# An attention stage whose engines take their work in the stated order

## Chip, cores and metric

The kernel runs on one core of one Trainium2 chip. The metric is the device time of one execution in microseconds. TensorE (PE) multiplies, VectorE (DVE) and ScalarE (ACT) do elementwise work, GpSimd (POOL) clears tiles, and SyncE (SP) issues the loads. The kernel before took 1140.14 us (median of three runs, 1138.94 to 1140.86).

## What is computed

One layer of a hybrid encoder on 256 frames of width 2048, in float32:

```
proj = x @ w_in                      # q | k | v | u, 1024 columns each
attn = chunk_band_attention(q, k, v) # 16 heads of 64; 64-frame chunks, own chunk and 8 before, a bias by distance
s_t  = a * s_(t-1) + B u_t           # 64 groups of 16 channels, a 64-dim complex diagonal state each
ssm  = Re(C s) + D u                 # then gelu, then ssm * sigmoid(ssm @ w_glu + b_glu)
x    = LN(alpha * x + concat(rms(attn), rms(ssm)) @ w_out)
x    = LN(alpha * x + (gelu(conv3(x @ W_gate)) * (x @ W_val)) @ w_ffn_out)
```

## The kernel before

Every large product is made in split form. A weight tile of 128 x 1024 float32 (a *chunk*, 512 KB) is loaded on SP's queue into `raw` (`dma_chunk`, four buffers); ScalarE rounds it to `hi`, VectorE makes `lo = raw - hi` (`split_chunk`, lines 163 and 164, four buffers each); TensorE multiplies hi and lo with activations split in the same way.

Phase 1 consists of 104 chunks, in this order: 0 to 7 half of v, 8 to 23 u, 24 to 31 the other half of v, 32 to 63 k and q (four chunks for each of eight head pairs j: two for k, two for q), 64 to 79 the half of the output projection (`oa`) that takes attention's output, 80 to 87 the gate of the state-space branch (`glu`), 88 to 103 the other half of the output projection (`os`). Phase 2 is the feed-forward part, 176 and 88 chunks.

`run` states the work in steps. Step j states the split of chunk j+3, the load of chunk j+7, the products of chunk j, what copies a finished result out (`evac_k`, `evac_q`: a ScalarE copy of one half and a VectorE addition), and then lets each *side* that has started go on to its next `yield`. Sides are Python generators with a first step; the ones that matter here are, in the order in which a step asks them:

- `s5_loc`, from step 16: the input products of the recurrence. For each of four groups of state columns (`pg`), `lt` transposes coefficients and `ll` (line 778) makes 32 small products of 64 columns; a ScalarE copy takes them into `X`.
- `s5_kstack`, from step 24: the correction products (line 873) and the table `Kt` made of them. `s5_cm`, from step 22: the output matrices `CM`, eight blocks of four VectorE operations (lines 943 to 948, the last doubled).
- `s5_scan`, from step 35: the recurrence in time, 21 complex multiply-adds (`madd`) of four VectorE operations each (lines 844 to 847). `paced` lets whole multiply-adds through until 1.6 us are reached per step. It ends with `s5_y`: four groups of output products (line 973, 32 x 64 pieces) and copies to `ysh`, then gelu and a split.
- `attention(j)`, one side for each head pair, from step 36 + 4j: scores (`S`, lines 1048 and 1049) from `kz` and `qt`, which have one buffer each; softmax (`soft`, VectorE lines 1061 and 1062, ScalarE line 1065); transposes (`T`, lines 1071 to 1073) and a ScalarE copy into `pT` (line 1075; a tile of a pool with one buffer); value products (`O`, lines 1084 to 1086); normalisation (`at`, line 1094, and ScalarE squares, line 1099); `evac`: transposes (line 1104), two ScalarE copies and a subtraction (lines 1108 to 1110) into `attnhl`, the split activations of the output projection. The bias tiles `band` come in two buffers.

Small products that are to fill TensorE's stream go through `queue`: `put(f, cost)` appends one, and `fill`, called between main products, earns one unit of credit (two at most) and takes products while it has a unit left. With cost 0.25 that is four at a time.

The stated order is not the order on the engines. Each instruction has a priority by its place, and a scheduler goes through a model of the engines' times: whenever an engine is free there, it takes the ready instruction of the best priority. So the recurrence, for one, can be put on VectorE earlier than it is stated. On the chip each engine then takes its list strictly in turn. An instruction can also be given an order edge (`add_manual_dep` without a semaphore), which fixes its place behind another one.

Of the kernel before, what the change touches and what calls it, by code (L numbers as in the profile page):

```python
# [34 lines left out]
NEG = -1e30  # L35

# [82 lines left out]
class Builder:  # L119
    def __init__(self, nc, tc, ctx, I, out):  # L120
        self.nc, self.tc, self.ctx, self.I, self.out = nc, tc, ctx, I, out
        self.chunks = []
        self.sides = []
        self.queue = deque()
        self.credit = 0.0
# [41 lines left out]
    def run(self, first=None):  # L167
# [11 lines left out]
        while j < len(self.chunks) or self.sides:  # L179
            self.split_chunk(j + 3)  # L180
# [15 lines left out]
            self.sides = keep  # L196
            j += 1

# [93 lines left out]
    def plan_phase1(self):  # L292
# [165 lines left out]
        self.side(35, self.s5_scan())  # L458
        for j in range(8):
            self.side(36 + 4 * j, self.attention(j))  # L460
# [291 lines left out]
    def s5_loc(self):  # L752
# [20 lines left out]
        def ll(q, ri):  # L773
# [11 lines left out]
            for i in range(8):  # L785
                for g2 in range(2):
                    put(lambda i=i, g2=g2: mm(i, g2), 0.25)
# [32 lines left out]
        both(ll, 2)  # L820
        both(ll, 3)
# [4 lines left out]
    def s5_scan(self):  # L826
# [8 lines left out]
        def madd(cost, o, s, ar, ai, shape, add=None):  # L835
# [4 lines left out]
            def f():  # L840
# [3 lines left out]
                V.tensor_tensor(u, s[:, ::-1], ai, op=ALU.mult)  # L844
                V.tensor_tensor(w, s, ar, op=ALU.mult)
                V.tensor_tensor(u, u, add, op=ALU.add)
                V.tensor_tensor(o, w, u, op=ALU.add)
            ops.append((cost, f))
# [4 lines left out]
        for k in range(2, 9):  # L853
            madd(2.7, row(k), row(k - 1), bc(QR, 0), bc(QI, 0), sh)
        for b in range(7):
            madd(1.1, X[:, :, :, 0, b + 1], X[:, :, :, 0, b], one(QR, 7), one(QI, 7), [P, 2, NP_], L8[:, :, :, b])
        for k in range(1, 8):
            madd(2.7, row(k), row(0), bc(QR, k - 1), bc(QI, k - 1), sh)
        yield from self.paced(ops, 1.6)
        yield from self.s5_y()  # L860

    def s5_kstack(self):
# [14 lines left out]
        for i in range(16):  # L877
            for ri in range(2):
                for h in range(2):
                    self.put(lambda i=i, ri=ri, h=h: mm(i, ri, h), 0.5)  # L880
# [71 lines left out]
    def s5_y(self):  # L952
        nc, bp = self.nc, self.bp
        X, Kt, CM, up = self.X, self.Kt, self.CM, self.up
        for pg in range(4):
# [5 lines left out]
            for f in range(2):  # L961
                for i in range(4):
                    m = slice(32 * i, 32 * i + 32)
                    for t in range(3):
                        for r in range(4):
# [7 lines left out]
                            nc.tensor.matmul(o, start=t == 0, stop=t == 2, tile_position=(0, 32 * r), **a)  # L973
                nc.vector.tensor_copy(ysh[:, 2 * pg + f].rearrange("p (b k i) -> p i k b", i=4, k=8),
# [61 lines left out]
    def attention(self, j):  # L1036
# [5 lines left out]
        def load(h):  # L1042
            b = st["b", h] = ap.tile([P, 256], F32, tag="band", bufs=2, name=f"bd{j}{h}")
            nc.sync.dma_start(b, I["band"][2 * j + h])

# [5 lines left out]
        def soft(h):  # L1051

            ps, b = st["S", h], st["b", h]
# [14 lines left out]
        def trans(h):  # L1068
            s = st["s", h]
            ps = self.bank(7, f"T{j}{h}")  # L1070
# [30 lines left out]
        def evac():  # L1101
# [7 lines left out]
            nc.scalar.copy(self.attnhl[:, j, 0:SEQ], a)  # L1109
# [279 lines left out]
```

## Time and profile before

| | us |
|---|---|
| median of three runs | 1140.14 |
| the profiled execution | 1141.15 |
| its span, first to last instruction | 1139.3 |
| busy: PE, DVE, ACT, POOL | 1110.3, 774.4, 566.6, 75.5 |
| mean granted TensorE clock | 0.991 |
| start of chunk 36 and of chunk 75 | 133.56, 301.04 |

In a row of a timeline the first number is the start in us from the span's start, the second the length, then engine, line, operation, out<-in by the program's names, shapes and a count; in brackets stands the idle time of the engine before it, and what ended that. Where a matmul's row is longer than the distance to the next start, the two overlap in the pipeline: the distance between starts is the price. A row of a table by stretches has the stretch, its length, the busy time of PE, PEld (weight loads), DVE, ACT and POOL with their instruction counts, the granted clock of TensorE (1.00 is full), the share of the DMA engines and GB/s. "[1.52 <-PE kq L209]" means that the engine was idle for 1.52 us and that a product of k or q at line 209 ended it.

### The profile page before, as it was taken

Reading aid. Unit: us, or ns where it says so; the run is one execution under the profiler, and the core shown is the slowest. Engines: PE = TensorE matmul, PEld = TensorE weight load, DVE = VectorE, ACT = ScalarE, POOL = GpSimd, SP = SyncE. Lnnn points to the kernel's source line nnn. Section 1 sums busy time; section 2 is a strip of 40 time slices with the busy share of each in tenths; the row PEclk is TensorE's granted clock in tenths of the full one; section 3 lists DMA queues with packets and bytes.
Section 4 is the critical chain, followed back from the end, with each engine's and each line's share of the span. In section 5 each row is a group of like instructions: output and inputs, shape, how many; then the busy total and the mean of one; then the engine's idle time right before and its main releaser. Section 6 shows DMA issues by size and latency. Waiting matters only on the chain.

```text
span 1139.3 us, 17905 instructions
## 1 busy us (share of the span) xinstructions
PE 1110.3 (97%) x6980; PEld 948.8 (83%) x6980; DVE 774.4 (68%) x1230; ACT 566.6 (50%) x882; POOL 75.5 (7%) x75
## 2 busy tenths in 40 slices
PE   8999979999999999999999999999999999999996
PEld 6887768888887888888888888888888888888885
DVE  7996889946588776666666666666666575454555
ACT  5455325537575565555555555555555443433350
POOL 2021300000011000000000000000000550000002
PEclk9999979999999999999999999999999999999998
DMA  8886334534766366666666666666666876666661
GB/s 303 279 226 164 118 122 139 162 96 138 244 188 201 108 204 186 185 188 185 188 188 188 186 187 186 186 185 185 189 186 187 307 223 197 190 198 190 192 195 74
DMA packets 61572, 212.03 MB, mean 186 GB/s; under 512 B 7344, under 2 KB 10800, under 8 KB 60592
## 3 DMA queue, kind: packets, MB, share of 16 engines
q1 hardware_dynamic: 59728, 204.18, 58.9%
q0 software_dynamic: 1472, 6.29, 1.8%
q8 instruction: 54, 0.88, 0.3%
q10 hardware_dynamic: 288, 0.43, 0.1%
q14 instruction: 30, 0.25, 0.1%
HBM read 207.46 MB, written 3.41 MB: 185 GB/s over the span
## 4 chain that ended last, share of the span: by engine, by line
PE 93%; DVE 4%; ACT 1%; issue 1%; DMA 1%; SPq 0%; POOL 0%; ACTq 0%; POOLq 0%
PE f L231 29%; PE f L224 15%; PE d L245 7%; PE d L249 7%; PE d L247 7%; PE kq L209 5%; PE u L209 2%; PE kq L211 2%; PE oa L249 1%; PE oa L245 1%; PE oa L247 1%; PE u L211 1%; PE glu L209 1%; DVE lo L164 1%; PE os L249 1%; PE os L245 1%
## 5 line engine op out<-in xcount | busy, mean ns | idle before, releaser
L164 DVE TENSOR_TENSOR lo<-raw,hi 128x1024 fp32r<-128x1024 f32 (+1 forms) x358 | 446.3, 1249 | 210.6 <-ACT hi L163 207.0
L163 ACT CAST hi<-raw 128x1024 fp32r<-128x1024 f32 (+1 forms) x358 | 374.3, 1047 | 300.0 <-PE d L249 116.9
L231 PE MATMUL f<-x1s,hi 128*128 128x512 f32 (+1 forms) x1408 | 487.2, 396 | 1.5 <-DVE x1s L1211 1.5
L224 PE MATMUL f<-x1s,lo 128*128 128x256 f32 x1408 | 380.0, 281 | 0.0
L231 PEld LDWEIGHTS f<-x1s,hi 128*128 128x128 f32 x1408 | 258.8, 188 | 57.6 <-DVE x1s L1211 1.8
L224 PEld LDWEIGHTS f<-x1s,lo 128*128 128x128 f32 x1408 | 265.8, 189 | 8.6
L247 PE MATMUL d<-lo,hid 128*128 128x512 f32 (+1 forms) x360 | 133.4, 371 | 0.0
L245 PE MATMUL d<-hi,hid 128*128 128x512 f32 (+1 forms) x360 | 133.4, 370 | 0.0
L249 PE MATMUL d<-hi,hid 128*128 128x512 f32 (+1 forms) x360 | 133.3, 370 | 0.0
L209 PE MATMUL kq<-xs,hi 128*128 128x512 f32 x240 | 92.8, 422 | 5.1 <-DVE qt L506 2.6
L247 PEld LDWEIGHTS d<-lo,hid 128*128 128x128 f32 x360 | 67.9, 188 | 11.7
L249 PEld LDWEIGHTS d<-hi,hid 128*128 128x128 f32 x360 | 67.8, 188 | 11.7
L245 PEld LDWEIGHTS d<-hi,hid 128*128 128x128 f32 x360 | 67.9, 188 | 11.5
L211 PE MATMUL kq<-xs,lo 128*128 128x256 f32 x240 | 69.8, 291 | 0.0
L209 PEld LDWEIGHTS kq<-xs,hi 128*128 128x128 f32 x240 | 47.0, 196 | 15.8 <-DVE qt L506 2.7
L1319 ACT COPY ga<-f 128x256 f32<-128x256 f32 x44 | 16.4, 372 | 83.3 <-PE f L231 83.3
L1326 DVE TENSOR_TENSOR gp<-f,ga 128x256 f32<-128x256 f32 x44 | 18.8, 426 | 45.6 <-ACT ga L1319 45.6
L1319 ACT COPY va<-f 128x256 f32<-128x256 f32 x44 | 16.4, 372 | 66.1 <-PE f L231 66.1
L1338 DVE TENSOR_TENSOR va<-f,va 128x256 f32<-128x256 f32 x44 | 18.7, 425 | 43.0 <-ACT va L1319 43.0
L211 PEld LDWEIGHTS kq<-xs,lo 128*128 128x128 f32 x240 | 47.2, 197 | 0.8
L209 PE MATMUL u<-xs,hi 128*128 128x512 f32 x120 | 43.5, 401 | 0.0
L1305 POOL DMA_DIRECT2D gb<-rows x4 | 2.2, 554 | 531.6 <-PE f L231 531.6
(228 smaller groups left out, 1366.9 us busy)
## 6 DMA issues: line engine op xcount, KB each, us to landing
raw<-wf SPq DMA_DIRECT2D x176, 512.0 KB, 3.7
raw<-wd SPq DMA_DIRECT2D x88, 512.0 KB, 4.1
raw<-wkq SPq DMA_DIRECT2D x32, 512.0 KB, 3.7
raw<-wo SPq DMA_DIRECT2D x32, 512.0 KB, 4.0
raw<-wu SPq DMA_DIRECT2D x16, 512.0 KB, 4.7
raw<-wv SPq DMA_DIRECT2D x15, 512.0 KB, 6.2
raw<-wg SPq DMA_DIRECT2D x8, 512.0 KB, 3.7
gb<-rows POOLq DMA_DIRECT2D x4, 1024.0 KB, 13.1
```

The source lines that it names most:

```text
L163: self.nc.scalar.copy(hi[:, c], raw[:, c])
L164: self.nc.vector.tensor_tensor(lo[:, c], raw[:, c], hi[:, c].bitcast(F32), op=ALU.subtract)
L209: nc.tensor.matmul(ps, start=first and kk == 0, stop=False, **h)
L211: nc.tensor.matmul(ps[:, 0:SEQ], start=False, stop=False, **l)
L224: nc.tensor.matmul(th(ps), lhsT=lo[:, w], rhs=th(x), start=False, stop=False)
L231: nc.tensor.matmul(ps[:, c], lhsT=hi[:, w], rhs=x[:, c], start=start and part is None, stop=stop)
L245: nc.tensor.matmul(ps, lhsT=ah, rhs=wh, start=first and kk == 0, stop=False)
L247: nc.tensor.matmul(ps, lhsT=ah, rhs=wl, start=False, stop=False)
L249: nc.tensor.matmul(ps, lhsT=al, rhs=wh, start=False, stop=last and kk == 1)
L1319: self.nc.scalar.copy(tv, v[:, :, 1])
L1326: nc.vector.tensor_tensor(g[:, 2:].rearrange("p (t c) -> p t c", t=2), p0, t, op=ALU.add)
L1338: nc.vector.tensor_tensor(tv, p0, tv, op=ALU.add)
```

## The change

In steps 36 to 73 every instruction of PE, DVE and ACT gets an order edge to the one stated before it on the same engine (`keep_order`, called at the end of each step), so that these three take their work as stated. SP and POOL are left to the scheduler. With it:

- The recurrence is spread out: single VectorE operations instead of whole multiply-adds, 1.2 us of them (0.68 or 0.28 each) per step up to step 63 and 2.4 from step 64. It is stated to end in step 69, and so the state's output products are stated in steps 70 to 73, among the chunks of the output projection.
- The 64-column products come in runs: the input products and the correction products cost 0 in the queue, the last two groups of input products are separated, and in `s5_y` both halves of a group are multiplied before the two copies.
- Attention's steps are drawn together: scores and softmax of both heads in the first step, both transposes two steps later (the second in bank 6, or 4 for the last pair), both value products and the normalisation in the next, then `evac`, its subtraction a step later. The bias tiles of a pair are loaded a pair ahead.

```diff
--- before.py
+++ after.py
@@ -33,6 +33,7 @@
 EPS = 1e-5
 ALPHA = 2.0 ** 0.25
 NEG = -1e30
+PINNED = 36, 74
 
 NPP = 8 + 8 + 8 + 16 + 16 + 44 * 4
 
@@ -122,6 +123,7 @@
         self.chunks = []
         self.sides = []
         self.queue = deque()
+        self.mark, self.last = None, {}
         self.credit = 0.0
 
 
@@ -177,6 +179,7 @@
         self.start()
         j = 0
         while j < len(self.chunks) or self.sides:
+            self.j = j
             self.split_chunk(j + 3)
             self.dma_chunk(j + 7)
             if j < len(self.chunks):
@@ -194,7 +197,28 @@
                         continue
                 keep.append(s)
             self.sides = keep
+            if first is not None:
+                self.keep_order(PINNED[0] <= j < PINNED[1])
             j += 1
+
+    def keep_order(self, on):
+
+        new, mark = [], self.mark
+        for i in reversed(self.nc.cur_bb.bb.instructions):
+            if i is mark:
+                break
+            new.append(i)
+        if new:
+            self.mark = new[0]
+        if not on:
+            return
+        for i in reversed(new):
+            if i.engine in (mybir.EngineType.PE, mybir.EngineType.DVE, mybir.EngineType.Activation):
+                prev = self.last.get(i.engine)
+                if prev is not None:
+                    self.tc.add_manual_dep(i, prev, mybir.DependencyInfo(
+                        mybir.DependencyClass.NoSync, mybir.DependencyReason.DATA), reason="order")
+                self.last[i.engine] = i.name
 
 
     def mm_a(self, ps, hi, lo, xs, k0, first, last, nk=8):
@@ -456,6 +480,7 @@
         self.side(24, self.s5_kstack(), 200)
         self.side(22, self.s5_cm())
         self.side(35, self.s5_scan())
+        self.side(30, self.first_band())
         for j in range(8):
             self.side(36 + 4 * j, self.attention(j))
         self.side(78, self.load_x())
@@ -784,7 +809,7 @@
                 nc.scalar.copy(self.L8[:, ri, q * 8:q * 8 + 8], v[:, :, 56:64])
             for i in range(8):
                 for g2 in range(2):
-                    put(lambda i=i, g2=g2: mm(i, g2), 0.25)
+                    put(lambda i=i, g2=g2: mm(i, g2), 0)
             put(evac, 0)
 
         def both(f, pg):
@@ -818,6 +843,7 @@
             yield
         yield
         both(ll, 2)
+        yield from drained()
         both(ll, 3)
         yield from drained()
         self.loc_done = True
@@ -841,22 +867,30 @@
                 u, w = (self.kcm[:, c:c + n].rearrange("p (r x) -> p r x", r=2) for c in (1024, 1536))
                 if len(shape) == 4:
                     u, w = (t.rearrange("p r (c b) -> p r c b", b=shape[3]) for t in (u, w))
-                V.tensor_tensor(u, s[:, ::-1], ai, op=ALU.mult)
-                V.tensor_tensor(w, s, ar, op=ALU.mult)
-                V.tensor_tensor(u, u, add, op=ALU.add)
-                V.tensor_tensor(o, w, u, op=ALU.add)
-            ops.append((cost, f))
+                return ((u, s[:, ::-1], ai, ALU.mult), (w, s, ar, ALU.mult), (u, u, add, ALU.add), (o, w, u, ALU.add))
+            for i in range(4):
+                def g(i=i):
+                    d, a, b, op = f()[i]
+                    V.tensor_tensor(d, a, b, op=op)
+                ops.append((cost, g))
         sh = [P, 2, NP_, 8]
         one = lambda q, k: q[:, :, :, k]
         bc = lambda q, k: one(q, k).unsqueeze(3).broadcast_to(sh)
         row = lambda k: L8 if k == 8 else X[:, :, :, k]
         for k in range(2, 9):
-            madd(2.7, row(k), row(k - 1), bc(QR, 0), bc(QI, 0), sh)
+            madd(0.68, row(k), row(k - 1), bc(QR, 0), bc(QI, 0), sh)
         for b in range(7):
-            madd(1.1, X[:, :, :, 0, b + 1], X[:, :, :, 0, b], one(QR, 7), one(QI, 7), [P, 2, NP_], L8[:, :, :, b])
+            madd(0.28, X[:, :, :, 0, b + 1], X[:, :, :, 0, b], one(QR, 7), one(QI, 7), [P, 2, NP_], L8[:, :, :, b])
         for k in range(1, 8):
-            madd(2.7, row(k), row(0), bc(QR, k - 1), bc(QI, k - 1), sh)
-        yield from self.paced(ops, 1.6)
+            madd(0.68, row(k), row(0), bc(QR, k - 1), bc(QI, k - 1), sh)
+        have = 0.0
+        for cost, f in ops:
+            while have < cost:
+                yield
+                have += 1.2 if self.j < 64 else 2.4
+            f()
+            have -= cost
+        yield
         yield from self.s5_y()
 
     def s5_kstack(self):
@@ -877,7 +911,7 @@
         for i in range(16):
             for ri in range(2):
                 for h in range(2):
-                    self.put(lambda i=i, ri=ri, h=h: mm(i, ri, h), 0.5)
+                    self.put(lambda i=i, ri=ri, h=h: mm(i, ri, h), 0)
         while self.queue:
             yield
         ps = st[0]
@@ -971,6 +1005,7 @@
                             else:
                                 a = dict(lhsT=CM[pg][:, t - 1, l, m], rhs=X[:, t - 1, pr])
                             nc.tensor.matmul(o, start=t == 0, stop=t == 2, tile_position=(0, 32 * r), **a)
+            for f in range(2):
                 nc.vector.tensor_copy(ysh[:, 2 * pg + f].rearrange("p (b k i) -> p i k b", i=4, k=8),
                                       ps[:, f * SEQ:(f + 1) * SEQ].rearrange("p (i k b) -> p i k b", i=4, k=8))
             yield
@@ -1039,10 +1074,6 @@
         v = self.res1
         st = {}
 
-        def load(h):
-            b = st["b", h] = ap.tile([P, 256], F32, tag="band", bufs=2, name=f"bd{j}{h}")
-            nc.sync.dma_start(b, I["band"][2 * j + h])
-
         def scores(h):
             ps = st["S", h] = self.bank(5 + h, f"S{j}{h}")
             nc.tensor.matmul(ps[:, 0:256], lhsT=qt[:, P:2 * P], rhs=kz[h], start=True, stop=True)
@@ -1050,7 +1081,7 @@
 
         def soft(h):
 
-            ps, b = st["S", h], st["b", h]
+            ps, b = st["S", h], self.band[j, h]
             s = ap.tile([P, 384], F32, tag="sT", bufs=2, name=f"sT{j}{h}")
             if h == 0:
                 st["m"] = ap.tile([P, 12], F32, tag="mx", bufs=2, name=f"mx{j}")
@@ -1067,7 +1098,7 @@
 
         def trans(h):
             s = st["s", h]
-            ps = self.bank(7, f"T{j}{h}")
+            ps = self.bank((7, 6 if j < 7 else 4)[h], f"T{j}{h}")
             nc.tensor.transpose(ps[:, 0:128], s[:, 256:384], self.ident)
             nc.tensor.transpose(ps[:, 128:256], s[:, 0:128], self.ident)
             nc.tensor.transpose(ps[:, 256:384], s[:, 128:256], self.ident)
@@ -1107,31 +1138,35 @@
             a = self.t1([P, SEQ], f"ag{j}")
             nc.scalar.mul(a, ps, self.pv["g_attn"][:, j:j + 1])
             nc.scalar.copy(self.attnhl[:, j, 0:SEQ], a)
+            yield
             nc.vector.tensor_tensor(self.attnhl[:, j, SEQ:], a, self.attnhl[:, j, 0:SEQ].bitcast(F32), op=ALU.subtract)
 
-        load(0)
-        load(1)
         scores(0)
         scores(1)
-        yield
         soft(0)
-        yield
         soft(1)
-        yield
         if j < 7:
-            yield
+            self.load_band(j + 1)
+        yield
+        yield
         trans(0)
+        trans(1)
         yield
         pv(0)
-        trans(1)
-        if j < 7:
-            yield
         pv(1)
         norm()
         yield
-        while self.cm_ready < 4:
-            yield
-        evac()
+        assert self.cm_ready == 4
+        yield from evac()
+
+    def load_band(self, j):
+        for h in range(2):
+            b = self.band[j, h] = self.ap_.tile([P, 256], F32, tag="band", bufs=2, name=f"bd{j}{h}")
+            self.nc.sync.dma_start(b, self.I["band"][2 * j + h])
+
+    def first_band(self):
+        self.band = {}
+        self.load_band(0)
         yield
 
 

```

More of the change, by code (lines that the diff above doesn't have):

```diff
@@ L1109, in evac @@
             nc.scalar.copy(self.attnhl[:, j, 0:SEQ], a)
+            yield
             nc.vector.tensor_tensor(self.attnhl[:, j, SEQ:], a, self.attnhl[:, j, 0:SEQ].bitcast(F32), op=ALU.subtract)
-        load(0)
-        load(1)
         scores(0)
         scores(1)
+        soft(0)
+        soft(1)
+        if j < 7:
+            self.load_band(j + 1)
         yield
-        soft(0)
         yield
-        soft(1)
-        yield
-        if j < 7:
-            yield
         trans(0)
+        trans(1)
         yield
         pv(0)
-        trans(1)
-        if j < 7:
-            yield
         pv(1)
```

## The prediction

> **What bounds the kernel now.** I read the stretches of the span first, then TensorE's timeline in the attention stage, then VectorE's and ScalarE's. A chunk below is one weight tile of the first phase, numbered in the stated order; chunks 32 to 63 make k and q, 64 to 79 are the attention half of the output projection. First the busy times by stretch (in this order: PE, PEld, DVE, ACT, POOL, then the granted clock, DMA share, GB/s):
>
> ```profile
> 146.48:183.48 37.00, 28.61 (x152) 23.76 (x152) 32.40 (x84) 12.60 (x31) 0.00 (x0) 0.82 0.34 100
> 183.48:227.38 43.90, 43.90 (x275) 39.01 (x273) 41.43 (x89) 26.41 (x70) 0.00 (x0) 1.00 0.54 165
> 227.38:257.77 30.39, 29.20 (x845) 24.95 (x845) 12.92 (x28) 11.52 (x20) 0.00 (x0) 1.00 0.31 98
> ```
>
> TensorE bounds nearly everything, but not the first stretch: there it is busy 28.61 of 37.00 us and the clock is at 0.82. VectorE is nearly full in two of the three stretches (32.40 of 37.00, 41.43 of 43.90) and well under half full in the third. The three long waits of the first stretch, in TensorE's timeline, and the clock behind the last of them:
>
> ```profile
> 152.36 0.80 PE L209 MATMUL kq<-xs,hi 128*128 128x512 f32 x1 [2.58 <-DVE qt L506]
> ...
> 163.03 0.33 PE L1071 MATMUL T<-ident,sT 128*128 128x128 f32 x1 [2.02 <-ACT sT L1065]
> ...
> 165.66 0.79 PE L209 MATMUL kq<-xs,hi 128*128 128x512 f32 x1 [2.09 <-DVE kz L501]
> ```
>
> ```profile
> 146.00:149.00 3.00, 2.38 (x30) 1.81 (x28) 2.92 (x7) 2.89 (x8) 0.00 (x0) 1.00 0.84 260
> ...
> 165.60:170.80 5.20, 5.14 (x16) 4.38 (x17) 3.94 (x9) 0.00 (x0) 0.00 (x0) 0.51 0.10 39
> ```
>
> All three end on attention's small VectorE or ScalarE operations, which stood behind recurrence steps that had been started early. With a granted clock of 0.51 the chunk at 165.66 runs at half speed; the row above it, for comparison, holds a wait of 0.62 us that left the clock at 1.00. So this stage has about 37.00 - 28.61 = 8.4 us of bare waiting, and a few us more of half clock, to give back.
>
> **Part 1: 64-column products in runs.** Today the input products of the recurrence (line 778) are issued four at a time between main products; once they came in one run:
>
> ```profile
> 118.58 0.40 PE L209 MATMUL kq<-xs,hi 128*128 128x512 f32 x1
> ...
> 119.71 0.45 PE L778 MATMUL ll<-up,loc 128*64 128x64 f32 x8
> ...
> 133.56 0.40 PE L209 MATMUL kq<-xs,hi 128*128 128x512 f32 x1
> ...
> 136.38 0.40 PE L209 MATMUL kq<-xs,hi 128*128 128x512 f32 x1
> ```
>
> ```profile
> 84.88 2.08 PE L778 MATMUL ll<-up,loc 128*64 128x64 f32 x64
> ```
>
> The rows at 118.58, 133.56 and 136.38 are the starts of chunks 34, 36 and 37. A k or q chunk alone takes 136.38 - 133.56 = 2.82 us. Chunks 34 and 35 with two interleaved groups took 133.56 - 118.58 = 14.98 us; the chunks themselves are 5.64 of it and two runs, at 2.0 each from the row at 84.88, would be 4.0. So the interleaving costs 5.3 us for two groups, 2.7 for one. Three of the four are interleaved today: 8.0 us; I take 7.2, since each run keeps a change in and out. TensorE then comes to chunk 36 at 133.56 - 7.2 = 126.4. The point to which I carry everything is the start of chunk 75, behind the pinned stretch (the row above it is that of chunk 74, so a chunk of the output projection takes 2.72):
>
> ```profile
> 298.32 0.39 PE L245 MATMUL oa<-hi,attnhl 128*128 128x512 f32 x1
> ...
> 301.04 0.39 PE L245 MATMUL oa<-hi,attnhl 128*128 128x512 f32 x1
> ```
>
> The correction products (cost 0.5 to 0) come in one run already, since they wait for a bank. The output products of the recurrence (line 973) lose the copy between their halves. They are in four runs afterwards and cost what they do now:
>
> ```profile
> 226.00:262.00 36.00, 13.49 (x752) 11.92 (x752) 1.00 0.29 89
> ```
>
> That is 13.5 us, or 13.49/752 = 18 ns a record. The Trainium skill (TensorE: Matmul & The Clock Gate, "Wait — 56ns, not 53.3ns?") gives a least distance of about 25 ns between matmul starts however few the columns are; by it these 752 would need 18.8 us and the forecast would be 5.3 us later. The row is below that rule, so the row decides.
>
> **Part 2: the order.** From chunk 36 to 73 PE, DVE and ACT take their instructions as written. Within a step j: ScalarE's hi and VectorE's lo of chunk j+3, the products, k's or q's copy-out, then the recurrence's share, then attention. VectorE may no longer jump over a waiting instruction. The steps of its queue (start to start), from rows of today:
>
> ```profile
> 158.14 1.05 ACT L163 CAST hi<-raw 128x1024 fp32r<-128x1024 f32 x1 [8.74 <-PE kq L209]
> ```
>
> ```profile
> 159.23 1.23 DVE L164 TENSOR_TENSOR lo<-raw,hi 128x1024 fp32r<-128x1024 f32 x1 [0.21 <-ACT hi L163]
> 160.37 0.68 DVE L847 TENSOR_TENSOR X<-kcm 128x512 f32<-128x512 f32 x1
> ```
>
> hi to lo 1.09, lo 1.14.
>
> ```profile
> 150.08 0.68 DVE L844 TENSOR_TENSOR kcm<-X,QI 128x512 f32<-128x512 f32 x1
> ...
> 151.89 0.42 DVE L506 SCALAR_TENSOR_TENSOR qt<-kq,qb 128x256 f32<-128x256 f32 x1
> 152.22 0.68 DVE L847 TENSOR_TENSOR X<-kcm 128x512 f32<-128x512 f32 x1
> ```
>
> Three recurrence operations in 1.81 us: 0.60 each; qt 0.33. A step gets 1.2/0.68 = 1.76 of them, 1.06 us.
>
> ```profile
> 175.49 0.85 DVE L501 TENSOR_TENSOR kz<-kq,kb 64x256 f32<-64x256 f32 x2
> 176.37 0.28 DVE L847 TENSOR_TENSOR X<-kcm 128x64 f32<-128x64 f32 x1
> ```
>
> ```profile
> 202.75 0.42 DVE L1094 TENSOR_TENSOR at<-O,mx 128x256 f32<-128x256 f32 x1
> 203.09 0.16 DVE L1062 TENSOR_SCALAR mx<-mx 128x2 f32<-128x2 f32 x1
> ```
>
> kz 0.88; at 0.34 to the next start, 0.42 to a reader, and the subtraction of attnhl, of the same shape, as much.
>
> ```profile
> 230.57 0.40 DVE L1061 CUSTOM_DVE_ANT_0 sT<-S,bd 128x256 f32<-128x256 f32 x1
> ...
> 231.23 0.17 DVE L1062 TENSOR_SCALAR mx<-mx 128x2 f32<-128x2 f32 x1
> ```
>
> Softmax start to its first exponential 0.66 + 0.17 = 0.83.
>
> ```profile
> 173.72 0.51 ACT L1065 ACTIVATE sT<-sT,mx 128x256 f32<-128x256 f32 x1 [1.76 <-DVE mx L1062]
> ...
> 174.61 0.35 ACT L467 COPY kb<-kq 128x256 f32<-128x256 f32 x1
> ...
> 175.81 0.31 ACT L1099 ACTIVATE aq<-at 128x128 f32<-128x128 f32 x1
> ...
> 176.40 0.36 ACT L469 ACTIVATE qb<-kq 128x256 f32<-128x256 f32 x1
> ```
>
> The exponentials take 0.89 a head, the squares 0.59.
>
> Now one head pair, four chunks, from `at` to the next `at`. The squares wait for `at`; behind them in ScalarE's queue stands hi of the next chunk, and behind that hi stands lo on VectorE: 0.42 + 0.59 + 1.09 = 2.10. Then lo 1.14, recurrence 1.06, softmax 0.83, two heads' exponentials 1.78, and the next hi, which stands behind these: 1.09. Then VectorE alone: lo 1.14, kz 0.88, recurrence 1.06, subtraction 0.34, lo 1.14, recurrence 1.06, lo 1.14, qt 0.33, recurrence 1.06, together 8.15. Sum 16.15, and 0.25 for the reciprocal and hand-overs (estimate from the 0.04 us between 159.19 and 159.23): **16.4 us**. VectorE works some 12.3 of them; the rest is the two places where it and ScalarE wait for one another in turn.
>
> TensorE needs less for the same pair. Today's steady cycle, from scores to scores:
>
> ```profile
> 193.80 0.60 PE L1048 MATMUL S<-kz,qt 128*128 128x256 f32 x2
> ...
> 208.48 0.60 PE L1048 MATMUL S<-kz,qt 128*128 128x256 f32 x2
> ```
>
> 14.68 us. One wait is added: both transposes now come a chunk ahead of the value products, but the tile pT has one buffer, so the second copy-out waits for the first head's value products and the second head's for that copy. The same round trip today:
>
> ```profile
> 148.00 0.27 PE L1073 MATMUL T<-ident,sT 128*128 128x128 f32 x1
> ...
> 148.90 0.43 PE L1084 MATMUL O<-vtok,pT 128*128 128x64 f32 x2 [0.62 <-ACT pT L1075]
> ```
>
> 0.90 from issue to issue where 0.11 would do: 0.79 more, so TensorE's own cycle is 15.5. Behind the waiting copy stand hi and qb; no main product needs them in that time. So the loop through VectorE, 16.4, is late next, and TensorE waits for it at the transposes of `at`.
>
> Where the loop starts: the output-matrix products (lines 943 to 948) run once the correction products let their buffer go, today from
>
> ```profile
> 116.02 0.69 DVE L943 TENSOR_TENSOR kcm<-prm 128x512 f32<-128x512 f32 x1
> ...
> 121.81 0.69 DVE L943 TENSOR_TENSOR kcm<-prm 128x512 f32<-128x512 f32 x1
> ...
> 124.55 0.69 DVE L943 TENSOR_TENSOR kcm<-prm 128x512 f32<-128x512 f32 x1
> ```
>
> 2.74 a block. Five blocks remain; all are now stated before chunk 36. In front of the first qt stand four (10.96), three lo (3.42), kz 0.88, and qt itself 0.33: 116.02 + 15.6 = 131.6. TensorE is there at 126.4 + 2.8 = 129.2 and waits 2.4 us: a third of the gain of part 1 goes here. Then the fifth block, lo and one recurrence operation: softmax at 136.1. From softmax to `at` is 16.4 - 4.3 - 0.34 = 11.8: the first `at` at 147.9, the seventh 6 x 16.4 later, at 246.3.
>
> **Part 3: the state's output behind chunk 70.** The recurrence ends in step 69, at double rate from step 64: 3.53 operations, 2.12 us a step. From the seventh `at` to the eighth: 2.10 + 1.14 + 2.12 + 0.83 + 1.78 + 1.09 = 9.1, then three lo, three shares and a subtraction, 10.1: 19.2 us. TensorE alone would be there after about 15.5, so it waits nearly 4 us. TensorE then does chunk 69 and most of chunk 70 and, at about 24.3, needs the last subtraction, which stands behind 2.10 + lo 1.14 + 2.12 + lo 1.14 + 0.6 and lasts 0.42: 26.7, a wait of 2.4. Behind that TensorE has 0.9 of chunk 70, 13.5 of output products, four chunks at 2.72 and 0.8 of changes: chunk 75 starts 53 us after the seventh `at`, at 299.3. Today it is 301.04. Gelu and the splits behind the last output product have chunks 75 to 79, 13.6 us, as cover; nothing later changes. The band loads move on SP behind a softmax that ends before the next weight load can start, so I cost them at nothing; without that cover it would be their 0.33 us of issue each.
>
> **Sum.** 301.0 - 299.3 = 1.7 us gained. The profiled execution took 1141.15 us with a span of 1139.3, so 1139.4 is what a profile of the same sort should take; the median of the runs is 1140.14, and I take the gain from the median: **1138.4 us**. The loop is good to about 0.5 us, over six turns 3; the tail to 2: 1134 to 1143 for this case.
>
> **The rivals.**
> - **TensorE stays the bound (faster).** If the in-order queues lose less than worked out, the cycle is TensorE's 15.5 and the tail loses its waits of nearly 4 and 2.4: 131.6 + 7 x 15.5 + 46.3 = 286.4, 14.6 us less: 1125.5. For it: nothing in today's rows shows VectorE held to an order, and 12.3 us of work would fit into 15.5. Against it: the sum of the loop, of which each link is a row. In-between values are as likely as the end.
> - **The clock falls in every pair (slower).** Two waits, 0.8 and 0.9 us, stand in each pair some 3.5 us apart. If they halve the clock as the waits of 2.02 and 2.09 us did, a chunk costs 5.2 us (the stretch at 165.60) instead of 2.8: 2.4 more, 0.9 of it under the loop's own wait, so 1.5 x 7 = 10.5 us more than the loop alone: 1149. The tail's longer waits cover what the clock does there. It decides from the point where such waits last some 1.5 us. Against it: the wait of 0.62 at 148.90 did not lower the clock by itself. The Trainium skill (TensorE: Matmul & The Clock Gate, "Why this matters for your kernels") asks for no gap above some 3 us; by it only the tail's wait would count, and the forecast stands.
> - **The order does not bind.** If the added edges change little, the early stalls stay and only part 1 counts: 7 us less, 1133.
>
> **How the numbers follow.** Chances: loop as worked out 0.50 (of it 0.20 faster, 0.22 same, 0.08 slower), TensorE bound 0.28, clock 0.14, order without effect 0.08. A measurement tells about 0.2%, 2.3 us, from no change. Faster 0.56, same 0.22, slower 0.22. The range 1122 to 1148 holds the loop, most of the TensorE case and the lower half of the clock case.
>
> **What would show it.** Right: cycle from scores to scores 16 to 17 us between chunks 40 and 64, TensorE's waits at line 1104 of the old kernel released by VectorE's `at`; second value products released by ScalarE's copy; long waits of 152 to 166 us gone, clock 1.00 there; chunk 36 some 7 us earlier; output products in four runs behind chunk 70. Wrong: a cycle under 15.7, hi or lo well ahead in it, or a clock below 1 in each pair.

## The result: slower by 0.4 to 0.7%

The changed kernel took 1148.38 us (median of four runs, 1144.81 to 1148.86) where the old one took 1140.01 beside it: a ratio of 1.0067 [1.0045, 1.0089]. A second series on another occasion gave 1144.97 (1144.35 to 1145.76) against 1140.72, 1.0039 [1.0026, 1.0052]. Both are slower by more than 0.2%; the forecast was 1138.4, faster, with a range of 1122 to 1148, and the first series lies just outside it.

The profiled execution took 1144.81 us with a span of 1143.0, 3.7 more than before. TensorE's timeline, a row for each point of the forecast (in brackets the idle time before it and what ended it):

```profile
126.33 0.40 PE L233 MATMUL kq<-xs,hi 128*128 128x512 f32 x1
...
131.19 0.67 PE L1079 MATMUL S<-kz,qt 128*128 128x256 f32 x2 [1.87 <-DVE qt L531]
...
164.14 0.44 PE L1135 MATMUL O<-ident,at 128*128 128x128 f32 x2 [0.90 <-DVE at L1125]
...
180.95 0.44 PE L1135 MATMUL O<-ident,at 128*128 128x128 f32 x2 [1.03 <-DVE at L1125]
...
246.21 0.80 PE L269 MATMUL oa<-hi,attnhl 128*128 128x512 f32 x1 [1.89 <-DVE qt L531]
...
267.34 0.44 PE L1135 MATMUL O<-ident,at 128*128 128x128 f32 x2 [1.92 <-DVE at L1125]
...
274.87 0.50 PE L273 MATMUL oa<-hi,attnhl 128*128 128x512 f32 x1 [2.53 <-DVE attnhl L1142]
...
304.71 0.39 PE L269 MATMUL oa<-hi,attnhl 128*128 128x512 f32 x1
```

Chunk 36 starts at 126.33, 7.2 us earlier than before; the first and last rows show that all of it and 3.7 more is lost by chunk 75 (304.71 against 301.04). Behind chunk 75 the two executions are alike: 1139.3 - 301.04 and 1143.0 - 304.71 are both 838.3. From the third row to the fourth is one head pair: 16.81 us.

All of TensorE's waits from 120 to 310 us (total us, times, longest):

```profile
PE O L1135 <- DVE at L1125: 6.9, 7, 1.9
PE O L1115 <- ACT pT L1106: 5.0, 8, 0.6
PE y L1007 <- issue: 4.4, 3, 1.7
PE oa L273 <- DVE attnhl L1142: 2.5, 1, 2.5
PE oa L269 <- DVE qt L531: 1.9, 1, 1.9
PE S L1079 <- DVE qt L531: 1.9, 1, 1.9
```

The early waits of before (2.6 + 2.5 + 2.4 = 7.5 us by the same view) are gone; in their place stand waits in every pair (the first two lines, 11.9 us), three single waits (the last three lines, 6.3 us), and three stops in the state's output products that nothing in the profile releases ("issue"). The timeline around these (tile `y`), with the second run, which has none, for comparison:

```profile
278.60 0.28 PE L1007 MATMUL y<-X,vtok 128*32 128x64 f32 x2
280.58 0.42 PE L1007 MATMUL y<-X,vtok 128*32 128x64 f32 x14 [1.70 <-issue]
...
283.89 0.36 PE L1007 MATMUL y<-up,Kt 128*32 128x64 f32 x8
...
286.86 0.50 PE L269 MATMUL oa<-hi,attnhl 128*128 128x512 f32 x1
...
291.49 0.29 PE L1007 MATMUL y<-up,Kt 128*32 128x64 f32 x3 [1.01 <-issue]
...
295.21 0.37 PE L1007 MATMUL y<-X,CM 128*32 128x64 f32 x11 [1.66 <-issue]
```

The second run takes 286.86 - 283.89 = 2.97 us. The four runs, each from its first product to the next main product, take 4.94, 2.98, 6.11 and 2.99: 17.0 us against 13.5 forecast. In the old kernel the same products stand in eight halves of about 1.4 to 1.8 us with other products between them, and one stop of 0.43 us is all:

```profile
227.38 0.43 PE L973 MATMUL y<-X,vtok 128*32 128x64 f32 x16
...
228.78 0.43 PE L1084 MATMUL O<-vtok,pT 128*128 128x64 f32 x2
...
230.78 0.35 PE L973 MATMUL y<-up,Kt 128*32 128x64 f32 x8 [0.20 <-DVE ysh L974]
...
251.04 0.29 PE L973 MATMUL y<-up,Kt 128*32 128x64 f32 x3 [0.43 <-issue]
```

The clock, by stretch (PE, PEld, DVE, ACT, POOL busy, then the granted clock, DMA share, GB/s):

```profile
147.00:231.00 84.00, 76.17 (x463) 66.51 (x464) 62.86 (x152) 42.97 (x113) 0.00 (x0) 1.00 0.47 142
...
246.00:250.00 4.00, 3.79 (x10) 2.99 (x11) 2.20 (x5) 1.63 (x5) 0.00 (x0) 0.57 0.49 149
```

It is full through the pairs and, between 126 and 306 us, falls only at the wait of chunk 64 (the row at 246.21).

Why the pairs take 16.8 us is seen on the two other engines, in the pair from 180.95 on. VectorE first, with the first softmax and the first, seventh and eighth `at`, then ScalarE:

```profile
132.98 0.42 DVE L1092 CUSTOM_DVE_ANT_0 sT<-S,bd 128x256 f32<-128x256 f32 x1
...
146.98 0.42 DVE L1125 TENSOR_TENSOR at<-O,mx 128x256 f32<-128x256 f32 x1
...
182.59 1.23 DVE L166 TENSOR_TENSOR lo<-raw,hi 128x1024 fp32r<-128x1024 f32 x1 [1.70 <-ACT hi L165]
...
188.04 1.23 DVE L166 TENSOR_TENSOR lo<-raw,hi 128x1024 fp32r<-128x1024 f32 x1 [2.07 <-ACT hi L165]
...
197.26 0.42 DVE L1125 TENSOR_TENSOR at<-O,mx 128x256 f32<-128x256 f32 x1
...
246.94 0.42 DVE L1125 TENSOR_TENSOR at<-O,mx 128x256 f32<-128x256 f32 x1
...
266.86 0.42 DVE L1125 TENSOR_TENSOR at<-O,mx 128x256 f32<-128x256 f32 x1
```

```profile
180.92 0.31 ACT L1130 ACTIVATE aq<-at 128x128 f32<-128x128 f32 x1 [3.58 <-DVE at L1125]
...
185.21 0.51 ACT L1096 ACTIVATE sT<-sT,mx 128x256 f32<-128x256 f32 x1 [1.84 <-DVE mx L1093]
...
192.44 0.48 ACT L1106 COPY pT<-T 128x384 f32<-128x384 f32 x1 [2.84 <-PE O L1117]
```

VectorE idles twice, 1.70 and 2.07 us, each time for hi, which stands in ScalarE's queue behind the squares and behind the exponentials. These are the two places that the forecast named. From 188.04 to `at` at 197.26 it has no idle time. ScalarE waits for VectorE before the squares (3.58) and before the exponentials (1.84). It has one more wait, 2.84 us for the buffer of the transposed scores.

### The profile page after: what moved, and what is told of

It reads as the page before. It is cut to its first block, busy times and chain, and to the rows that moved or that the text cites. A ratio compares the mean times of both kernels' runs of the same rounds, so it can differ in the third digit from the quotient of the medians.

```text
span 1143.0 us, 17911 instructions
## 1 busy us (share of the span) xinstructions
PE 1100.8 (96%) x6980; PEld 944.2 (83%) x6980; DVE 772.9 (68%) x1230; ACT 562.9 (49%) x880; POOL 76.5 (7%) x75
## 3 DMA queue, kind: packets, MB, share of 16 engines
HBM read 207.46 MB, written 3.41 MB: 184 GB/s over the span
## 4 chain that ended last, share of the span: by engine, by line
PE 74%; DVE 1%; issue 1%; ACT 0%; POOL 0%; ACTq 0%; POOLq 0%
PE f L255 29%; PE f L248 15%; PE d L269 7%; PE d L273 7%; PE d L271 7%; PE glu L233 1%; PE os L273 1%; PE y L1007 1%; PE os L269 1%; PE os L271 1%; PE oa L269 1%; PE oa L273 1%; PE oa L271 1%; PE glu L235 1%; PE f L250 0%
## 5 line engine op out<-in xcount | busy, mean ns | idle before, releaser
L233 PE MATMUL kq<-xs,hi 128*128 128x512 f32 x240 | 87.2, 402 | 0.3 <-DVE kz L526 0.3
L235 PE MATMUL kq<-xs,lo 128*128 128x256 f32 x240 | 67.3, 280 | 0.0
L1354 ACT COPY va<-f 128x256 f32<-128x256 f32 x44 | 16.4, 372 | 66.1 <-PE f L255 66.1
```

Source lines behind the costliest of these rows:

```text
L233: nc.tensor.matmul(ps, start=first and kk == 0, stop=False, **h)
L235: nc.tensor.matmul(ps[:, 0:SEQ], start=False, stop=False, **l)
L1354: self.nc.scalar.copy(tv, v[:, :, 1])
```

## The experiments

Each was measured beside the old kernel; "chunk 75" is its start in the profile.

**The parts alone.** The change without its order edges, and the old kernel with nothing but the runs:

```diff
-PINNED = 36, 74
+PINNED = 0, 0
```

> The changed kernel without its order edges; all else of the change stays. Loop theory (in the stated order VectorE and ScalarE wait for one another in turn, 16.4 us for a head pair, and TensorE waits for them): the pair's cycle falls to about 15, the waits on VectorE's `at` go, and the time falls by 5 us or more against the changed kernel, to 1143 or less; the output products still stop for instructions. Rival, the one pT buffer sets the cycle: the cycle stays above 16 wherever both transposes still come ahead of the value products, and the time stays within 3 us of 1148. Rival, the order itself was worth something: the early waits of some 2 us each come back and the time rises above 1150.

Measured: 1129.63 us, 0.9901 [0.9887, 0.9914], chunk 75 at 289.83. As the loop theory said, a pair takes (238.97 - 149.59)/6 = 14.90 us from `at` to `at`, and of the waits for `at` 0.4 us is left.

```diff
-                    put(lambda i=i, g2=g2: mm(i, g2), 0.25)
+                    put(lambda i=i, g2=g2: mm(i, g2), 0)
...
+        yield from drained()
         both(ll, 3)
...
-                    self.put(lambda i=i, ri=ri, h=h: mm(i, ri, h), 0.5)
+                    self.put(lambda i=i, ri=ri, h=h: mm(i, ri, h), 0)
...
+            for f in range(2):
                 nc.vector.tensor_copy(ysh[:, 2 * pg + f].rearrange("p (b k i) -> p i k b", i=4, k=8),
```

> The kernel before with the product runs alone (cost 0 in the queue, last two groups separated, both halves of an output group before their copies). If the runs are worth what part 1 says, chunk 36 starts some 7 us earlier; as VectorE was nearly full from 116 us on, most of that is lost in waits behind it: 1133 to 1139. Rival, runs of output products run out of instructions: their runs show stops of 1 to 2 us each with no releaser and cost 2 to 5 us of it: 1136 to 1142.

Measured: 1126.91 us, 0.988 [0.9865, 0.9895], chunk 75 at 287.01. This is below both expected ranges: the gain of part 1 isn't lost behind chunk 36. So the runs are a gain of 14 us by themselves, and the order edges cost the changed kernel 15 us (1144.97 - 1129.63). Later only the first two edits of these, those of the input products, were left:

> The old kernel with the recurrence's input products in runs and the last two groups separated, and nothing else: no edit of the correction and of the output products. The run with all three edits took 1126.9. Theory: the input products are its whole gain (7 to 9 us before chunk 36, and the three early waits of 2.0 to 2.6 us with their half clock, which go because TensorE no longer runs behind the recurrence there): 1125 to 1129. Rival, the correction products or the output products have a share: 1131 or more.

Measured: 1124.61 us, 0.986 [0.9847, 0.9874], chunk 36 at 125.21 and chunk 75 at 284.68. The theory holds: the input products are the whole gain, and the two other edits add nothing to it (1126.91; the stops that they bring are dealt with below). 8.4 us of it are there at chunk 36 (133.56 - 125.21), and 8.0 more by chunk 75 (301.04 - 284.68 = 16.4): the early waits shrink without any order. TensorE's waits in this kernel, 120 to 310 us:

```profile
PE T L1072 <- ACT sT L1066: 2.5, 1, 2.5
PE kq L211 <- DVE lo L164: 0.9, 1, 0.9
PE y L974 <- issue: 0.8, 2, 0.6
PE y L974 <- DVE ysh L975: 0.7, 2, 0.4
```

Of the early 7.5 us 2.5 are left. The forecast's third rival ("the early stalls stay and only part 1 counts") had priced this at 1133.

**Which order costs.** Edges on TensorE alone:

```diff
-            if i.engine in (mybir.EngineType.PE, mybir.EngineType.DVE, mybir.EngineType.Activation):
+            if i.engine in (mybir.EngineType.PE,):
```

> The changed kernel with order edges on TensorE alone. Loop theory: VectorE and ScalarE may pass a waiting instruction, the cycle falls to TensorE's own 15.3 to 15.7 with only the pT wait left, and the time falls to 1136 to 1143. Rival, pT buffer: the cycle stays at 16.4 or more and the time within 3 us of 1148.

Measured: 1143.73 us, 1.003 [1.0016, 1.0043]. TensorE's order alone is as dear: its waits for `pT` rise to 9.1 us in eight and the first scores wait 6.3 for `qt`. Why is not shown. A miss: this does not isolate VectorE's and ScalarE's order.

**The two loops of a pair.** First the places where VectorE idles: the exponentials are stated a step later behind the next hi, the squares likewise.

```diff
-            for t, a, e in spans:
+            st["s", h] = s
+
+        def expo(h):
+            s, m = st["s", h], st["m"]
+            for t, a, e in ((1, 0, 256), (0, 256, 384)):
...
+        def squares():
+            a = st["a"]
...
         yield
+        expo(0)
+        expo(1)
         yield
         trans(0)
...
+        squares()
         yield from evac()
```

> The changed kernel with ScalarE's exponentials and squares stated one step later, behind the next chunk's hi; nothing is left out, the order edges stay. Loop theory: hi no longer stands behind work that waits for VectorE, so the two queues do not wait in turn: the cycle falls from 16.6 to 15.3 to 15.6 (TensorE with the pT wait), the waits on `at` and the stop in chunk 64 nearly go, chunk 75 starts 8 to 14 us earlier, time 1134 to 1141. Rival, pT buffer sets the cycle: nothing changes, 16.4 or more, time within 3 us of 1148. Rival, clock: the time follows the granted clock and not the cycle.

Measured: 1143.70 us, 1.0022 [1.0012, 1.0033], where 1134 to 1141 was expected: a pair still takes (247.99 - 149.91)/6 = 16.35 us. ScalarE's, VectorE's and TensorE's timelines of this kernel show why:

```profile
195.13 0.48 ACT L1109 COPY pT<-T 128x384 f32<-128x384 f32 x1 [3.34 <-PE O L1120]
...
196.59 1.23 DVE L166 TENSOR_TENSOR lo<-raw,hi 128x1024 fp32r<-128x1024 f32 x1 [2.88 <-ACT hi L165]
...
200.25 0.44 PE L1141 MATMUL O<-ident,at 128*128 128x128 f32 x2 [0.87 <-DVE at L1128]
```

VectorE's idle time is now in one place, 2.88 us. The second head's copy into the single `pT` buffer waits for the first head's value products; hi stands behind that copy, lo behind hi, and qt, two recurrence operations and `at` behind lo. That is a second loop, through TensorE's value products back to TensorE's transposes of `at`. Taking only this one away, the copy going back into the score tile that has just been transposed (it has two buffers):

```diff
-            pt = st["pt", h] = ap.tile([P, 384], F32, tag="pT", name=f"pT{j}{h}")
+            pt = st["pt", h] = s
```

> The changed kernel, but the copy-out of a head's transposes goes back into that head's own score tile, so the second copy no longer waits for the first head's value products. In the profile of the changed kernel ScalarE waits 2.84 us for them in each pair, and TensorE 0.62 before the second value products. Loop theory (VectorE and ScalarE wait for one another behind the squares and behind the exponentials, 1.70 and 2.07 us of a pair's 16.8): this round trip lies beside the loop, TensorE's 0.62 moves into its wait for the normalised output, the cycle stays 16.2 to 16.8 and the time stays within 2 us of the changed kernel's 1148. Rival, the single buffer of the transposed scores sets the cycle: it falls to 14.7 to 15.3 and the time by 8 us or more.

Measured: 1145.26 us, 1.0038 [1.0025, 1.005]. As the loop theory said, the time is that of the second series of the changed kernel (1144.97), and a pair still takes (245.45 - 145.17)/6 = 16.71 us: the 5.0 us of waits for `pT` are gone, and those for `at` have risen from 6.9 to

```profile
PE O L1135 <- DVE at L1125: 11.3, 6, 2.7
```

Either edit alone is worth 1 us or nothing. Both together:

> The kernel with the exponentials and squares stated later, and with the transposes' copy going back into the score tile. Each of the two alone leaves a loop: in the run with the later squares ScalarE waited 3.34 us for the first value products, and behind that copy stood hi, lo (VectorE idle 2.88), qt, the recurrence and the normalisation. If these two loops lie within half a microsecond of one another, as worked out from the traces, both edits together give TensorE's own cycle, 14.7 to 15.2, a start of chunk 64 of 232 to 236 instead of 243.2, and 1131 to 1137 us. Rival, a third bound (VectorE's work in stated order, about 12.3 us plus hand-overs) is as late: the cycle stays above 15.8 and the time above 1140.

Measured: 1128.95 us (1126.15 to 1131.32), 0.9901 [0.9886, 0.9916], 2 us below the expected range. All of TensorE's waits from 120 to 310 us in this kernel, and a stretch of its table:

```profile
PE y L1007 <- issue: 5.0, 3, 2.0
PE S L1079 <- DVE qt L531: 3.3, 1, 3.3
PE oa L273 <- DVE attnhl L1148: 0.5, 1, 0.5
```

```profile
147.00:221.00 74.00, 74.00 (x464) 66.18 (x463) 63.84 (x154) 43.73 (x110) 0.00 (x0) 1.00 0.53 161
```

TensorE is busy for 74.00 of 74.00 us, with as many products as the changed kernel made in 84.00 (464 and 463), and a pair takes 14.77 (191.34 - 176.57, from rows of the same kind as above). Two loops of nearly the same length (16.71 with the second removed, 16.35 with the first) lay on top of one another; each hid what removing the other would bring.

**The stops in the output products.** A `yield` between the halves of a group, so that half as many small products stand together:

```diff
+                if f == 0:
+                    yield
             for f in range(2):
                 nc.vector.tensor_copy(ysh[:, 2 * pg + f].rearrange("p (b k i) -> p i k b", i=4, k=8),
```

> The changed kernel, but a step takes half a group of the state's output products, so that 192 small products and weight loads stand between chunks instead of 384, in steps 70 to 77. Supply theory (the stops of 1.70, 1.01 and 1.66 us with no releaser stand at every 256th instruction, since a run of 384 small instructions goes through two blocks of instructions in 3 us while a block takes about 1 us to be fetched): the stops vanish or fall below 0.4 us each, eight half runs at 1.5 to 1.7 us are 12 to 13.5 instead of 17.0, and the time falls by 3 to 5 us to 1143 to 1146. Rival, the stops belong to the data or the bank of these products: they stay with the same groups, the sum stays above 16 us and the time within 1.5 us.

Measured: 1143.13 us, 1.002 [1.0011, 1.0029]. No wait for "issue" is left in its profile; the eight half runs take 1.56 to 1.59 us each, 12.6 together, 4.4 less than 17.0. Of this 3.4 us are left at chunk 79 (312.24, in the changed kernel 315.59), with four more changes between small and large products, and 2.1 in the span (1140.9, from 1143.0): a wait of 0.9 us for the state's split comes in ahead of the gate's first product (chunk 80), as the last half now stands closer to its use. In the old kernel chunk 79 starts at 311.92, so without the stops the changed kernel is still no faster. The supply theory holds, and four further findings support it. First, counted over TensorE's matmuls and weight loads in order of start, the stops of the changed kernel fall on records 3733, 4245 and 4501, which are 2 x 256 and 256 apart; in all eleven profiles with such stops, old kernel included, they fall on a remainder of 147 to 167 of 256, whichever product that is (some records are missing from each trace). Second, the page of the changed kernel has these lines:

```profile
PE 1100.8 (96%) x6980; PEld 944.2 (83%) x6980; DVE 772.9 (68%) x1230; ACT 562.9 (49%) x880; POOL 76.5 (7%) x75
...
q8 instruction: 54, 0.88, 0.3%
```

13,960 records over 54 packets are 258.5 a packet, and 0.88 MB over 54 is 16.3 KB. Third, in each of the 24 stops of these eleven profiles a packet of the instruction queue (q8) had started 2.2 to 2.8 us before the products went on, and took 0.9 to 1.4 us; in the changed kernel they start at 278.08, 289.14 and 292.80. Fourth, a run without a stop passes 384 records in 2.97 us, 256 in 2.0, which is less than these 2.2 to 2.8 us, while a k or q chunk has 32 in 2.8. The Trainium skill (Runtime: NRT & Kernel Launch, "Instruction fetch mechanics") says that instructions come in 16 KiB blocks of 256, and that crossing a boundary is mostly hidden. The block agrees with the rows; the second part doesn't in such a run, where a stop lasted 0.7 to 2.6 us.

The same edit on the old kernel with all runs:

> The old kernel with the 64-column products in runs (1126.9), and with the output products of the recurrence in half groups between chunks. Its output products took about 16.2 us in four runs, 5.3 and 4.7 in the first and third. Supply theory: 12 to 13.5 us for the eight half runs, so 1122.5 to 1125. Rival (stops belong to the data or the bank): 1126 to 1128. As both kernels lose their stops by the same edit, this one is to be the fastest so far.

Measured: 1123.84 us (1123.29 to 1124.66), 0.985 [0.9837, 0.9864], the lowest median of all; its profile has no such stop.

**The wait of chunk 64.** The first block of the output projection takes banks 0 and 7, the last pair's transposes 3 and 4:

```diff
-                    b0 = ((0, 1), (5, 6))[nb % 2]
+                    b0 = (0, 7) if nb == 0 else ((0, 1), (5, 6))[nb % 2]
...
-            ps = self.bank((7, 6 if j < 7 else 4)[h], f"T{j}{h}")
+            ps = self.bank((7, 6)[h] if j < 7 else (3, 4)[h], f"T{j}{h}")
```

> The changed kernel, but the first block of the output projection takes banks 0 and 7 instead of 0 and 1, so that chunk 64 no longer waits for the last q to leave bank 1 (1.89 us in the profile, and a clock of 0.52 behind it). Loop theory: the VectorE loop of 19.9 us ends at the eighth normalised output in any case, so the wait moves to the evacuation of the last pair (1.92 before, 3.5 to 4 then), chunk 75 starts within 1 us of 304.7, and the time is within 2 us of the changed kernel's. Rival, the lost clock delays what the loop needs: 3 us or more faster.

Measured: 1146.54 us, 1.0056 [1.0042, 1.007], chunk 75 at 305.68. The wait at chunk 64 is gone and the clock is full there, but TensorE stops at the last pair's transposes instead (the longest wait for `at` is 3.5 us, 1.9 in the changed kernel), and the low clock has moved with it:

```profile
246.00:250.00 4.00, 2.97 (x16) 2.26 (x15) 2.47 (x5) 1.36 (x5) 0.00 (x0) 1.00 0.62 238
262.00:276.00 14.00, 10.54 (x36) 8.21 (x36) 12.15 (x20) 5.25 (x11) 0.00 (x0) 0.76 0.40 114
```

From chunk 64 to chunk 75 it takes 305.68 - 244.61 = 61.07 us, the changed kernel 304.71 - 243.38 = 61.33, and the seventh `at` lies 19.91 us before the eighth, in the changed kernel 19.92. So that wait, with the half clock behind it, lay under the loop's cover. (What this kernel lost at the start, 1.2 us by chunk 64, has no part in that.)

**The changed kernel again, and with all its waits mended.**

> The changed kernel again, nothing edited. Its profiled execution took 1144.81 us at a mean granted clock of 0.996, its other three 1147.95 to 1148.86 at 0.990 to 0.992. Theory: the stops of TensorE are the same in each execution, and what differs is for how long the clock falls behind the waits of 1 to 2 us in chunks 40 to 75; then executions of about 1148 have a clock of 0.992 or below, those of about 1145 one near 0.996, and a profile of one of the former shows stretches behind such waits at a clock of about a half which the profile at 0.996 does not have. Rival: the difference lies elsewhere in the span, so that chunk 75 still starts at 304.7 within 1 us.

Measured: 1144.97 us, five executions of 1144.35 to 1145.76 with clocks from 0.993 to 0.996, chunk 75 at 304.93. The theory about the clock is not borne out: 1144.35 had a clock of 0.993, less than the 0.996 of 1144.97, and the run with other banks had 0.992 at 1144.86. Why three executions of the first series took some 3 us more stays open; no profile shows one of them.

> The changed kernel with three edits: exponentials and squares stated later, the transposes' copy back into the score tile, output products in half groups. The first two gave 1128.95 with stops of 5.0 us in the output products; half groups took 17.0 down to 12.6, and the last of them stands two steps before gelu's result is needed, which cost a wait of 1.0 us. So 1124 to 1126: the order itself costs nothing once its waits are gone, but it gains nothing either over the old kernel in runs and half groups (1123.84). Rival, the order has a cost or a gain of its own: over 1128 or under 1122.

Measured: 1124.45 us (1122.96 to 1125.86), 0.9858 [0.9845, 0.9872]. With the three edits (later exponentials and squares, `pT` in the score tile, half groups) the order costs nothing, and gains nothing over the old kernel in runs (1123.84, 1124.61).

## Why the prediction was wrong

- **Part 1, input runs: right.** Chunk 36 at 126.33 (126.4).
- **First `qt`: right.** The scores start at 131.19 (131.6), after an idle time of 1.87 us (2.4).
- **The loop: right in mechanism and size.** (246.94 - 146.98)/6 = 16.66 us a pair (16.4), idle at both named places, seventh `at` at 246.94 (246.3), eighth at 266.86 (246.3 + 19.2 = 265.5). That it holds the cycle is shown by two runs together: with only the other loop removed a pair takes 16.71 us, with both 14.77. The first `at` at 146.98 (147.9) is right by luck: the softmax before it started at 132.98, not 136.1, and 14.00 us lie between the two, not 11.8, so that misses of 3.1 and 2.2 us nearly cancel. One statement in it was wrong: that behind the waiting copy into `pT` "no main product needs" hi. Products didn't, but VectorE's lo did, and `at` behind it: what was put at 15.5 us for TensorE is a loop of 16.35 us. It changed nothing here, as the other loop was a little longer; it hid the remedy.
- **The last subtraction: right.** A wait of 2.53 us (2.4), 1.9 us late (274.87, forecast 273.0).
- **The output products: the step that failed.** "They are in four runs afterwards and cost what they do now." The row of 13.5 us is the price of eight halves with a copy and other work between them, which the change took away; in four runs they cost 17.0, 4.4 of it in three stops for instructions. This is 3.5 us of the 5.4 by which chunk 75 missed its forecast (304.71, not 299.3). Of the other 1.9, 1.4 were there at the eighth `at`: the first was 0.9 early, the six turns 1.6 longer, the last one 0.7.
- **The sum.** With 17.0 in it the forecast would have been 302.8, 1.8 us slower than before: in the forecast the sign hung on this one term, as the loop had eaten the gain of the runs. On the chip it did not hang on it alone: with half groups, at 12.6 us, the kernel is still slower (1.0020).
- **From profile to median.** 3.7 us slower by the profile became 4.3 in the second series and 8.4 in the first, whose last 4 us are not explained.
- **The rivals.** "TensorE stays the bound" did not happen, but its 1125.5 is near what the kernel takes once both loops and the stops are gone (1124.45); that is in part luck, as it counted 15.5 us a pair where 14.77 were measured. "The clock falls in every pair" is refuted by the clock of 1.00 from 147 to 231 us, in spite of waits of 0.6 and 0.9 us in each pair; by that the rule of the Trainium skill cited there (TensorE: Matmul & The Clock Gate: no gap above some 3 us) holds for the pairs. "The order does not bind" took the early stalls for something that only the order can mend; the input runs alone removed most of them.

## What to carry to other kernels

An order fixed on all engines turns each wait into a wait of everything queued behind it: work out the loops through all queues, list every loop within a few per cent of the longest, and remove them together, since one alone shows nothing. Try each part of a change by itself: here one edit (input products in runs) held all of the gain, and the rest gave it back. Hundreds of tiny products in one run can outrun the supply of instructions (here 384 records in 3 us), so break such runs up with larger work. And where a cost is taken over from today's row, ask whether the change keeps what stood between the parts of that row.

## What the runs showed of the hardware

- A run of 384 small TensorE instructions in 3 us stopped for 0.7 to 2.6 us at some of the points that lie 256 records apart. In halves of 192 with other work between them for some 3 us or more none did, in the three kernels that had them; with less between them (old kernel, input runs alone) three stops of 0.2 to 0.6 us were left.
- The clock did not follow the length of a single wait: 1.89 us before chunk 64 left it at 0.57, while 1.92 us at 267.34 and 2.53 us at 274.87 left it full (1.00 in the stretches 262 to 276 and 276 to 306 of the same view). The rule of the Trainium skill (TensorE: Matmul & The Clock Gate, "Why this matters for your kernels"), no gap above some 3 us, does not foresee the first. What tells them apart is where they lie. In each of the fourteen profiles the granted clock changes only at times that are whole multiples of 3.41 us apart (in the old kernel at 150.19, 157.02, 163.85 and 170.68). Cut into these steps, the first wait lies almost whole in one step, and the next one has half the clock; the two others are each cut in two:

```profile
242.70:246.11 3.41, 1.61 (x9) 1.14 (x9) 3.34 (x6) 1.16 (x2) 0.00 (x0) 1.00 0.50 147
246.11:249.52 3.41, 3.31 (x8) 2.64 (x9) 1.61 (x5) 1.63 (x5) 0.00 (x0) 0.50 0.56 165
263.18:266.59 3.41, 2.24 (x10) 1.50 (x8) 3.41 (x5) 0.00 (x0) 0.00 (x0) 1.00 0.44 139
266.59:270.00 3.41, 2.66 (x13) 2.25 (x14) 1.62 (x4) 2.65 (x8) 0.00 (x0) 1.00 0.29 115
270.00:273.42 3.42, 2.34 (x11) 1.61 (x9) 3.38 (x6) 2.94 (x3) 0.00 (x0) 1.00 0.50 153
273.42:276.83 3.41, 1.96 (x59) 1.51 (x63) 2.77 (x6) 0.47 (x2) 0.00 (x0) 1.00 0.50 139
```

The wait of 1.87 us before the first scores is the same in the changed kernel and in the run with other banks. In the latter it lies whole in the step from 127.82 to 131.24, and the next step has half the clock; in the changed kernel it is cut at 130.06, and the clock stays full. Over the fourteen profiles, from 20 to 310 us, each of the 18 steps at full clock in which TensorE was idle for 1.87 us or more was followed by half the clock. Of the 1130 with less, four were: the one above (1.80 us) and three with 1.0 to 1.2. What sets these apart from the others, one of which had 1.83, is open.
